# Values of the decode rows: plain float32 products, four batches to four quarters of the PSUM partitions

## The chip, the cores and the metric

The kernel runs on one core of a Trainium2 chip. The time is the device time of one execution in microseconds (us), and lower is better. Three executions were timed and one more was profiled.

## What is computed

One layer of a hybrid decoder is run on a prompt of 1024 tokens and on 32 decode rows (8 batches of 4 new tokens). Both go through one input projection, a state-space branch with a gated linear unit, and an attention branch of 8 heads of 64 columns; the two branches are normalised and multiplied by `w_out`. The part that matters here is the attention of the decode rows over the cached keys and values, which is three dilated windows for each new token:

```python
def _dilated_gather(q, k_all, v_all, window, dil):
    ...
    kg = k_all[:, idx_c]
    vg = v_all[:, idx_c]
    s = jnp.einsum('bthe,btkhe->bhtk', q, kg) * (HEAD_DIM ** -0.5)
    ...
    p = jnp.exp(s - m[..., None])
    l = jnp.sum(p, axis=-1)
    o = jnp.einsum('bhtk,btkhe->bthe', p, vg)
    return o, m.transpose(0, 2, 1), l.transpose(0, 2, 1)
```

All inputs and results are float32.

## The kernel before

TensorE multiplies in a fast reduced form, float32r. To keep accuracy the kernel splits most operands into a high part (ScalarE copies into a float32r tile) and a low part (VectorE or GpSimd subtract the high part from the source), and adds up two or three products of parts. Names that end in `h` and `l`, or `hi` and `lo`, are such parts. A few small products are done on plain float32 tiles instead.

The program has four stages: the input projection with the state-space blocks; the gated unit with the decode rows' scores; a stretch in which three jobs are mixed; and a last stage in which the attention half of the output projection is done for eight slices of the prompt. The change is in the third stage, whose three jobs are:

- The prompt's attention heads, 8 of them. For each, TensorE makes scores (`ss`, L1518), VectorE adds a mask and finds row extremes (`pm`, `mn`, L1521), ScalarE takes exponentials (L1533), GpSimd divides (L1541), TensorE transposes (`tp`, L1560), ScalarE and VectorE make parts (`ph`, L1564, and `pl`, L1567), and TensorE multiplies them with the values (`ops`, L1575). A head has 10 micro steps of transposes and products.
- The ssm half of the output projection (`fo`, L1670), 32 groups of 6 matmuls.
- The values of the decode rows, in `values_ops`. For each of 8 batches there are 6 tiles of 128 cached rows by 512 columns (`ct`, 256 KB each), loaded from `cache_v` by `cache_tile`. ScalarE makes `vh` (L1355), VectorE and GpSimd in turn make `vl` (L1359), and TensorE multiplies the softmax weights `st6` of this batch and tile with both (L1365). The weights hold high and low parts side by side: 2 parts x 4 tokens x 8 heads are 64 columns, so that a batch's result is 64 x 512 in a PSUM bank. A product makes all 8 heads' columns for each head's weights; `mask` (L1377) keeps the right ones, `pick` (L1381) adds up two batches' rows with the constant matrix `selb` into a 32 x 512 tile, and VectorE adds that to `yad` (L1386).

The order of instructions on TensorE, VectorE, ScalarE and GpSimd in this stage is that of `Plan.run`: each step has an engine, a cost in microseconds, a priority, steps that it depends on, and tokens (buffers) that it takes and gives. A list schedule over these costs gives the order in which the steps are written. `CT`, `VH` and `VL` are the numbers of `ct`, `vh` and `vl` buffers. SyncE (the queue `SP`) issues all transfers in the order of the program; the transfers' engine is `DM` in the plan. The softmax weights `st6` are written in `decode_ops` by `his`, `los` and `far` before the values begin; zeros in them are set by GpSimd.

Of the kernel before, what the change touches and what calls it, by code (L numbers as in the profile page):

```python
# [103 lines left out]
def hymba_kernel(ctx: ExitStack, tc: tile.TileContext, I, O):  # L104
# [29 lines left out]
    def f(t):  # L134
        return t.bitcast(F32)
# [974 lines left out]

    CT, VH, VL, LEAD = 5, 2, 1, 6
    d3 = ExitStack()
    early = maskp = d2 = hmask = st6 = yad = sc = None

    def open_decode():
        nonlocal early, maskp, d2, hmask, st6, yad, sc
        rst.close()
        dst.close()
        fin[0] = None
        early = ctx.enter_context(tc.tile_pool(reuse_waits="tile", name="early", bufs=1))  # L1120
        maskp = early.tile([128, 1024], F32, name="maskp")
        SY.dma_start(maskp, I["c_maskp"])
        d2 = dec[0] = dst.enter_context(tc.tile_pool(reuse_waits="tile", name="d2", bufs=1))
        hmask = d2.tile([128, 512], F32, name="hmask")
        SY.dma_start(hmask, I["c_hmask"])
        st6 = d2.tile([128, 6, DB, 2, DS, H], F32R, name="st6")
        yad = d2.tile([NT, 512], F32, name="yad")
        sc = d3.enter_context(tc.tile_pool(reuse_waits="tile", name="d3", bufs=1)).tile([64, DS, 292], F32, name="sc")

    def decode_ops(t0, dt_, opened):  # L1130
# [10 lines left out]
        o.q, o.k, o.v = newr  # L1141
        z6 = op(PO, 1.8, lambda: GP.memset(f(st6[:, 2:6]), 0.0), t0, [opened])
        shn = [64, 2, DS, E]
# [77 lines left out]
        def his(k):  # L1221
            def fn():
                if k == 0:
                    S.activation(by_batch(st6[:, 0, :, 0]), o.pv, AF.Copy)
                else:
                    for j in range(DS):
                        S.activation(st6[:, 2 + j, :, 0, j, :], o.pv[:, j], AF.Copy)
            return fn

        def los(k):  # L1230
            def fn():
                if k == 0:
                    V.tensor_tensor(out=by_batch(st6[:, 0, :, 1]), in0=o.pv, in1=f(by_batch(st6[:, 0, :, 0])), op=OP.subtract)
                else:
                    for j in range(DS):
                        V.tensor_tensor(out=st6[:, 2 + j, :, 1, j, :], in0=o.pv[:, j], in1=f(st6[:, 2 + j, :, 0, j, :]), op=OP.subtract)
            return fn

        for k in range(2):
            step(PE, 0.2, turn(k), take=["fo"])  # L1240
            step(AC, 0.4 + 0.5 * k, his(k), deps=[last[0], z6])
            step(VE, 0.4 + 0.2 * k, los(k), give=["fo"])

# [9 lines left out]

        def far():
            o.far = row()[:, :256].rearrange("p (j n) -> p j n", j=DS)
            V.tensor_tensor(out=o.far, in0=o.p.unsqueeze(1).to_broadcast([128, DS, 64]),
                            in1=sel3.unsqueeze(2).to_broadcast([128, DS, 64]), op=OP.mult)
            o.far = o.far.rearrange("p j (b h) -> p j b h", h=H)
        step(VE, 0.3, far, give=["fo"], take=["dm"])
        step(AC, 0.4, lambda: S.activation(by_batch(st6[:, 1, :, 0]), o.far, AF.Copy))  # L1260
        step(VE, 0.4, lambda: V.tensor_tensor(out=by_batch(st6[:, 1, :, 1]), in0=o.far, in1=f(by_batch(st6[:, 1, :, 0])), op=OP.subtract),
             give=["dm"])
        return o

    def own_ops(o, t0):
# [3 lines left out]
        def own(u):  # L1269
            def fn():  # L1270
                if u == 0:
                    o.on = gk([128, 512], "vh", bufs=VH)[:64, :256].rearrange("p (j e) -> p j e", e=E)
                r = slice(2 * u, 2 * u + 2)
# [63 lines left out]
    def values_ops(t0, dt_, own, sel):  # L1337

        o = Box()
        o.c, o.vh, o.vl, o.po = {}, {}, {}, {}  # L1340
        end = own
        prev = lows = None
        for b in range(DB):
            if b % 2 == 0:
                w = Box()
            for t in range(6):
                n = 6 * b + t
                pr = t0 + n * dt_

                def load(b=b, t=t, n=n):  # L1350
                    o.c[n] = cache_tile(cv, b, t)

                def vhi(n=n):
                    o.vh[n] = gk([128, 512], "vh", F32R, VH)
                    S.activation(o.vh[n], o.c[n], AF.Copy)  # L1355

                def vlo(n=n, e=GP if n % 2 else V):
                    o.vl[n] = gk([128, 512], "vl", F32R, VL)
                    e.tensor_tensor(out=o.vl[n], in0=o.c[n], in1=f(o.vh[n]), op=OP.subtract)  # L1359

                def mm(b=b, t=t, n=n):
                    if t == 0:
                        o.po[b] = fo_ps([64, 512])
# [4 lines left out]
                a = op(DM, 0.75, load, pr - 2, [], take=["ct"])  # L1368
                a = op(AC, 0.52, vhi, pr - 0.5, [a], take=["vh"])
                lows = op(PO if n % 2 else VE, 1.23 if n % 2 else 0.6, vlo, pr - 0.5, [a, lows if VL == 1 else None], take=["vl"], give=["ct"])  # L1370
                prev = op(PE, 0.43, mm, pr, [lows, prev], take=["fo"] if t == 0 else [], give=["vh", "vl"])


            def mask(b=b, w=w):
                if b % 2 == 0:
                    w.m = row()
                V.tensor_tensor(out=w.m[64 * (b % 2):64 * (b % 2) + 64], in0=o.po[b], in1=hmask[:64], op=OP.mult)  # L1377

            def pick(g=b // 2, w=w):
# [3 lines left out]
            a = op(VE, 0.6, mask, pr, [prev], take=[] if b % 2 else ["dm"], give=["fo"])  # L1383
            if b % 2:
                a = op(PE, 0.85, pick, pr, [a, sel], take=["kt"], give=["dm"])
                end = op(VE, 0.6, lambda w=w: V.tensor_tensor(out=yad, in0=w.yd, in1=yad, op=OP.add), pr, [a, end], give=["kt"])  # L1386

        def zin():
            o.z, o.g = row(NT), gk([128, 512], "vh", bufs=VH)[:NT]
            SY.dma_start(o.z, d_pd.rearrange("j b c -> (j b) c")[:, 2560:3072])  # L1390
# [34 lines left out]

    selb = gp.tile([128, DB // 2, NT], F32, name="selb")

# [221 lines left out]
    def out_ssm_ops(t0, dt_):  # L1649
# [3 lines left out]
        for s in range(8):  # L1653
# [9 lines left out]
            for u in range(2):  # L1663
                for hf in range(2):
# [22 lines left out]

    plan.tokens = {**BANKS, "pp": 8, "ct": CT, "vh": VH, "vl": VL, "dm": 1, "nv": 1, "ko": 1, "q": 3, "ka": 2,
                   "vs": 2, "mn": 4, "dn": 4, "rd": 4, "ph": 2, "yp": 3, "gt": 1, "st": 2, "gh": 2,
# [91 lines left out]
def _constants():  # L1781
# [18 lines left out]
    col = np.arange(NT)[None, None, :]  # L1800
    batch = 2 * np.arange(DB // 2)[None, :, None] + r[:, None, None] // 64
    selb = ((r[:, None, None] // 8 % 4 == col // 8) & (batch == col % 8)).astype(np.float32)
# [81 lines left out]
```

## Time and profile before

| what | value |
|---|---|
| time, median of 3 runs | 741.25 us (740.29 to 742.72) |
| the profiled execution's own time | 745.36 us |
| its span in the profile | 743.6 us |
| TensorE busy in the span (PE) | 683.3 us, 92% |
| VectorE (DVE) | 564.1 us, 76% |
| ScalarE (ACT) | 366.8 us, 49% |
| GpSimd (POOL) | 348.0 us, 47% |
| mean transfer rate | 159 GB/s |

A busy share of TensorE includes the time in which a matmul runs out of its pipeline while the next one is already in it, so 92% is not 92% of its peak. PEld is the weight load of TensorE, which overlaps its matmuls. Times in the rows below are from the start of the span.

### The profile page before, as it was taken

The page shows a single profiled execution, that of the slowest core. Times are in us where ns is not written, and L with a number is a line of the kernel's source. Part 1 is how long each engine was busy: PE and PEld are TensorE (multiplying, and loading weights), DVE is VectorE, ACT ScalarE, POOL GpSimd, SP SyncE. Part 2 cuts the span into 40 slices and gives each one's busy share as a digit, 9 for nine tenths or more (in the row PEclk, how much of TensorE's full clock was granted, in tenths as well). Part 3 has the DMA queues.
Part 4 walks back from the last instruction along what each step waited for, and adds up shares of the span by engine and source line. Part 5 has one row for each costly group of instructions (what it writes and reads, how often), then busy time and mean ns, then how long its engine had stood idle before and what let it go on. Part 6 is the DMA issues. An engine that isn't in the chain of part 4 may idle for free.

```text
span 743.6 us, 12795 instructions
## 1 busy us (share of the span) xinstructions
PE 683.3 (92%) x4286; PEld 623.8 (84%) x4286; DVE 564.1 (76%) x1249; ACT 366.8 (49%) x814; POOL 348.0 (47%) x315
## 2 busy tenths in 40 slices
PE   7999989779798899999899999889999989898995
PEld 5999979679798889999899899668777768786995
DVE  5997858777978687346687687598899999974584
ACT  6663242514234355244343324277788878762442
POOL 2326456445564632203575750056788778430041
PEclk9999988979899999999989999999999999997998
DMA  8612432222224243277866745598998686116032
GB/s 280 202 57 82 145 99 76 78 95 61 73 90 126 80 153 94 92 248 259 261 203 186 243 135 193 161 298 275 262 300 242 202 254 178 41 58 229 19 120 114
DMA packets 78034, 118.38 MB, mean 159 GB/s; under 512 B 15216, under 2 KB 43376, under 8 KB 77968
## 3 DMA queue, kind: packets, MB, share of 16 engines
q1 hardware_dynamic: 77968, 117.56, 50.0%
q8 instruction: 34, 0.56, 0.3%
q14 instruction: 32, 0.26, 0.1%
HBM read 85.73 MB, written 30.62 MB: 156 GB/s over the span
## 4 chain that ended last, share of the span: by engine, by line
PE 51%; DVE 24%; DMA 8%; issue 6%; ACT 5%; POOL 5%; SPq 1%; DVEq 0%; POOLq 0%; ACTq 0%
PE mm L314 13%; PE mm L294 6%; PE fo L1670 4%; PE ss L294 3%; PE tp L294 3%; PE ops L1575 3%; DVE pm L1521 3%; POOL dm L977 3%; PE so L685 3%; PE tp L1560 2%; DVE vl L1359 2%; PE ss L1518 2%; DVE pl L1567 2%; PE fo L1365 2%; DVE win L143 2%
## 5 line engine op out<-in xcount | busy, mean ns | idle before, releaser
L314 PE MATMUL mm<-xT,win 128*128 128x352 f32 x1008 | 178.1, 334 | 15.1 <-DVE eq L381 13.7
L314 PEld LDWEIGHTS mm<-xT,win 128*128 128x128 f32 x1008 | 168.2, 196 | 16.8 <-issue 14.0
L1022 PE MATMUL mm<-xT,win 128*128 128x352 f32 x432 | 76.4, 331 | 0.4 <-DVE win L1004 0.2
L977 POOL TENSOR_TENSOR dm<-ct,dq 128x512 f32<-128x512 f32 x40 | 52.8, 1350 | 46.6 <-DMA ct<-in_cache_k_dram 27.6
L1022 PEld LDWEIGHTS mm<-xT,win 128*128 128x128 f32 x432 | 70.5, 192 | 1.1 <-DVE win L1004 0.9
L1541 POOL TENSOR_SCALAR pm<-pm,rd 128x128 f32<-128x128 f32 (+3 forms) x64 | 51.0, 803 | 32.2 <-DVE rd L1537 27.7
L1533 ACT ACTIVATE pm<-pm,mn 128x128 f32<-128x128 f32 (+3 forms) x64 | 49.3, 772 | 13.2 <-DVE mn L1521 12.1
L294 PE MATMUL mm<-win,xT 128*128 128x256 f32 x384 | 51.7, 290 | 0.1
L1567 DVE TENSOR_TENSOR pl<-tp,ph 128x512 fp32r<-128x512 f32 (+1 forms) x80 | 49.4, 627 | 3.0 <-ACT ph L1564 2.9
L1670 PE MATMUL fo<-wo,gh 128*128 128x512 f32 x192 | 51.0, 406 | 0.3 <-DVE yp L1597 0.3
L809 PE MATMUL gl<-yh,wg 128*128 128x272 f32 (+1 forms) x256 | 50.8, 297 | 0.0
L294 PEld LDWEIGHTS mm<-win,xT 128*128 128x128 f32 x384 | 48.1, 194 | 0.5 <-ACT xT L139 0.4
L1564 ACT ACTIVATE ph<-tp 128x512 fp32r<-128x512 f32 (+1 forms) x80 | 43.1, 547 | 8.1 <-PE tp L1560 7.0
L1560 PE MATMUL tp<-ident,pm 128*128 128x128 f32 x288 | 45.1, 275 | 0.5 <-DVE mn L1521 0.5
L143 DVE SCALAR_TENSOR_TENSOR win<-wst,gin,win 128x256 fp32r<-128x256 f32 x72 | 43.9, 650 | 1.9 <-ACT win L142 1.4
L809 PEld LDWEIGHTS gl<-yh,wg 128*128 128x128 f32 x256 | 41.9, 198 | 0.0
L1670 PEld LDWEIGHTS fo<-wo,gh 128*128 128x128 f32 x192 | 35.4, 193 | 7.4 <-DVE yp L1597 0.6
L1521 DVE CUSTOM_DVE_ANT_0 pm<-ss,maskp 128x512 f32<-128x512 f32 (+2 forms) x64 | 36.6, 580 | 6.0 <-PE ss L1518 5.9
L1560 PEld LDWEIGHTS tp<-ident,pm 128*128 128x128 f32 x288 | 34.4, 141 | 6.4 <-DVE mn L1521 1.4
L980 DVE TENSOR_REDUCE scd<-dm 128x8 f32<-128x512 f32 x40 | 26.9, 680 | 15.9 <-POOL dm L977 15.8
L1518 PE MATMUL ss<-ka,qt 128*128 128x512 f32 (+2 forms) x96 | 36.1, 378 | 2.5 <-DMA ka<-d_k 1.8
L809 PE MATMUL gl<-yl,wg 128*128 128x272 f32 (+1 forms) x128 | 37.6, 294 | 0.0
(411 smaller groups left out, 1648.6 us busy)
## 6 DMA issues: line engine op xcount, KB each, us to landing
wst<-in_w_in_dram SPq DMA_DIRECT2D x24, 512.0 KB
ct<-in_cache_k_dram SPq DMA_DIRECT2D x48, 256.0 KB
ct<-in_cache_v_dram SPq DMA_DIRECT2D x48, 256.0 KB
xt<-in_x_prompt_dram SPq DMA_DIRECT2D x8, 512.0 KB
wst<-in_w_out_dram SPq DMA_DIRECT2D x8, 512.0 KB
xres<-in_x_prompt_dram SPq DMA_DIRECT2D x8, 512.0 KB
qt<-d_q SPq DMA_DIRECT2D x16, 256.0 KB
qw<-d_q SPq DMA_DIRECT2D x32, 128.0 KB
```

The source lines that it names most:

```text
L143: V.scalar_tensor_tensor(lo, src, scale, f(hi), op0=OP.mult, op1=OP.subtract)
L294: T.matmul(out, lhs(a, kt), w(b, kt)[:, c0:c0 + cn], start=(n == 0), stop=(n == 3 * ktn - 1))
L314: T.matmul(p, w(b, kt)[:, c * 128:c * 128 + 128], x(a, kt), start=(n == 0), stop=(n == 23))
L809: T.matmul(p, wg[:, b, kt, c:c + 128], o.y[a][:, kt, :, :o.w], start=(n == 0), stop=(n == 11))
L977: GP.tensor_tensor(out=y.m, in0=y.c, in1=x.q, op=OP.mult)
L1022: T.matmul(x.p, o.w[kt][:, b, c * 128:c * 128 + 128], xT[a][:, kt, 352 * k:352 * k + 352], start=(kt == 0 and j == 0), stop=(kt == 7 and j ...
L1518: T.matmul(x.p[c][:, :w], q[:, i % 4 * 128:i % 4 * 128 + 128], o.ka[:, 512 * c:512 * c + w], start=(m == 0), stop=(m == 1))
L1521: V.tensor_tensor_reduce(out=x.pm[:, 512 * c:512 * c + w], in0=x.p[c][:, :w], in1=maskp[:, (7 - i) * 128 + 512 * c:(7 - i) * 128 + 512 * c ...
L1541: a = op(PO, 0.02 + n * 0.0012, lambda: GP.tensor_scalar(x.pm[:, :n], x.pm[:, :n], x.rd, 1.0, op0=OP.mult, op1=OP.mult), pr, [a], give=["rd"])
L1560: T.transpose(x.p[:, n * 128:n * 128 + 128], o.rows[2 * m + u].pm[:, j * 128:j * 128 + 128], ident)
L1567: V.tensor_tensor(out=x.l[:, :w], in0=x.p[:, :w], in1=f(x.h[:, :w]), op=OP.subtract)
L1670: T.matmul(o.f[hf], o.g[u][:, i, k], wo[0][:, j, 2 * u + k, hf * 512:hf * 512 + 512], start=(u + k + n == 0), stop=(u + k + n == 4))
```

## The change

The softmax weights `st6` are kept in one part, as plain float32: 4 tokens x 8 heads are 32 columns for a batch and tile. The values tiles are multiplied as they come, without `vh` and `vl`. Four batches are taken together: batch 4g + b writes partitions 32b to 32b + 31 of one PSUM bank, so that there are 2 groups of batches with 6 tiles each, 12 steps of four products, in place of 48 steps of two. `mask` now works on 128 partitions, and there are 2 masks, picks and additions in place of 8, 4 and 4. `selb` and its constant follow. `CT` goes from 5 to 8, and the tokens of `vl` are gone.

```diff
-    CT, VH, VL, LEAD = 5, 2, 1, 6
+    CT, LEAD = 8, 6
...
-        st6 = d2.tile([128, 6, DB, 2, DS, H], F32R, name="st6")
+        st6 = d2.tile([128, 6, DB, DS, H], F32, name="st6")
...
-            step(VE, 0.4 + 0.2 * k, los(k), give=["fo"])
+            step(AC, 0.4 + 0.5 * k, his(k), deps=[last[0], z6], give=["fo"])
...
-        step(AC, 0.4, lambda: S.activation(by_batch(st6[:, 1, :, 0]), o.far, AF.Copy))
-        step(VE, 0.4, lambda: V.tensor_tensor(out=by_batch(st6[:, 1, :, 1]), in0=o.far, in1=f(by_batch(st6[:, 1, :, 0])), op=OP.subtract),
-             give=["dm"])
...
-                def vhi(n=n):
-                    o.vh[n] = gk([128, 512], "vh", F32R, VH)
-                    S.activation(o.vh[n], o.c[n], AF.Copy)
...
-                    e.tensor_tensor(out=o.vl[n], in0=o.c[n], in1=f(o.vh[n]), op=OP.subtract)
...
-                    for u, x in enumerate((o.vh[n], o.vl[n])):
-                        T.matmul(o.po[b], st6[:, t, b].rearrange("p u j h -> p (u j h)"), x,
-                                 start=(t == 0 and u == 0), stop=(t == 5 and u == 1))
...
-                prev = op(PE, 0.43, mm, pr, [lows, prev], take=["fo"] if t == 0 else [], give=["vh", "vl"])
...
+                        w.po = fo_ps([128, 512])
+                    for b in range(4):
+                        T.matmul(w.po[32 * b:32 * b + 32], st6[:, t, 4 * g + b].rearrange("p j h -> p (j h)"), o.c[b, t, g],
+                                 start=(t == 0), stop=(t == 5))
+
+                prev = op(PE, 2.2, mm, pr, [*loads, prev], take=["fo"] if t == 0 else [], give=["ct"] * 4)
...
+                V.tensor_tensor(out=w.m, in0=w.po, in1=hmask, op=OP.mult)
```

On TensorE, at the first values products of the stretch, the order before is this (a pair of products for one tile, between pieces of the first head; `wo` and `gh` are the output projection):

```order
L1575 MATMUL ops<-pl,vs 128x256 x2
L1365 MATMUL fo<-vh,st_5314 64x512
L1365 MATMUL fo<-vl,st_5314 64x512
L1560 MATMUL tp<-ident,pm_5714 128x128
...
L1670 MATMUL fo<-wo_4987,gh 128x512 x6
L1365 MATMUL fo<-vh,st_5314 64x512
L1365 MATMUL fo<-vl,st_5314 64x512
L1518 MATMUL ss<-ka,qt 128x512
```

And this is the order of the changed program around its first pick, that is from the end of the first half of the batches to the second step of the second half (L1340 is the values product, L1352 the pick, L1640 the projection, L1488 the scores):

```order
L1352 MATMUL kt<-dm,selb 32x512
L1340 MATMUL fo<-ct,st_5314 32x512 x4
L1640 MATMUL fo<-wo_4987,gh 128x512 x6
L1488 MATMUL ss<-ka,qt 128x512
L1488 MATMUL ss<-ka,qw 128x512
L1640 MATMUL fo<-wo_4987,gh 128x512 x6
L1488 MATMUL ss<-ka,qt 128x128
L1488 MATMUL ss<-ka,qw 128x128
L1340 MATMUL fo<-ct,st_5314 32x512 x4
```

Products that came in pairs all through the stretch now come four at a time. The last values product stood behind 61 of the 80 micro steps, and stands behind 33 of them now; the projection groups ahead of it were 24 of 32 and are 15.

On SyncE's queue, from the first values load, the order before is this (`qt`, `qw` and `ka` are a head's queries and keys, `nv` its values, `d_h` a store of projected rows):

```order
L890 DMA ct<-in_cache_v_dram 128x512
L1463 DMA ka<-d_k 128x512
L892 DMA ct<-in_cache_v_dram 128x1x512
L1453 DMA qt<-d_q 128x512
L1454 DMA qw<-d_q 64x512
L1455 DMA qw<-d_q 64x512
L894 DMA ct<-in_cache_v_dram 128x512
```

And in the changed program, from the same place:

```order
L890 DMA ct<-in_cache_v_dram 128x512 x4
L1433 DMA ka<-d_k 128x512
L1423 DMA qt<-d_q 128x512
L1424 DMA qw<-d_q 64x512
L1425 DMA qw<-d_q 64x512
L1667 DMA selb<-in_c_selb_dram 128x64
L892 DMA ct<-in_cache_v_dram 128x1x512 x4
L1433 DMA ka<-d_k 128x512
L1414 DMA nv<-d_v 128x1024
L1656 DMA d_h<-xres 128x512
L894 DMA ct<-in_cache_v_dram 128x512 x4
```

Four loads stand together now, one for each batch of a group, and the loads of a head stand between such fours.

## Rows read from the trace of the kernel before

**Rows 1.** Windows: busy us (and instructions) of each engine, granted clock, transfers.

```profile
core 0: us, PE busy (x) PEld busy (x) DVE busy (x) ACT busy (x) POOL busy (x), PEclk, DMA share, GB/s
472.10:492.50 20.40, 17.09 (x84) 13.31 (x83) 15.15 (x44) 10.22 (x25) 8.24 (x10) 1.00 0.88 260
492.50:565.00 72.50, 68.85 (x421) 56.69 (x419) 64.19 (x161) 56.45 (x121) 51.15 (x44) 1.00 0.92 280
565.00:640.00 75.00, 71.23 (x433) 56.69 (x433) 71.85 (x179) 60.81 (x131) 59.35 (x54) 1.00 0.67 202
640.00:665.20 25.20, 22.78 (x145) 20.19 (x143) 23.28 (x63) 18.15 (x39) 8.95 (x9) 0.93 0.12 34
665.20:679.00 13.80, 10.92 (x59) 9.51 (x59) 4.70 (x8) 3.07 (x6) 1.30 (x1) 0.82 0.27 91
679.00:743.60 64.60, 56.98 (x225) 52.40 (x224) 37.66 (x100) 25.13 (x59) 11.10 (x8) 0.92 0.33 123
```

**Rows 2.** TensorE's groups by line, 472 to 680 us: busy, mean ns | idle before.

```profile
L1670 PE MATMUL fo<-wo,gh 128*128 128x512 f32 x192 | 51.0, 406 | 0.3 <-DVE yp L1597 0.3
L1560 PE MATMUL tp<-ident,pm 128*128 128x128 f32 x288 | 45.1, 275 | 0.5 <-DVE mn L1521 0.5
L1518 PE MATMUL ss<-ka,qt 128*128 128x512 f32 (+2 forms) x96 | 36.1, 378 | 2.5 <-DMA ka<-d_k 1.8 <-DMA qt<-d_q 0.5 <-DVE mn L1521 0.2
L1575 PE MATMUL ops<-pl,vs 128*128 128x256 f32 (+1 forms) x160 | 34.8, 300 | 1.7 <-DVE pl L1567 1.6
...
L1381 PE MATMUL kt<-dm,selb 128*32 128x512 f32 x8 | 4.2, 604 | 0.0
L1630 PE MATMUL kt<-ones,sq 128*64 128x1 f32 x32 | 4.2, 259 | 3.2 <-DVE sq L1625 3.2
```

**Rows 3.** Pieces of the chain of waits: start us, us, what.

```profile
515.92 0.46 PE ss L1518 x2
516.38 0.46 PE ops L1575 x4
517.17 0.47 PE fo L1365 x2
665.21 2.08 PE kt L1630 x16
671.37 2.75 PE fo L1670 x12
```

**Rows 4.** TensorE in order of time around a pick: start us, us.

```profile
529.10 0.60 PE L1560 MATMUL tp<-ident,pm 128*128 128x128 f32 x4
...
530.23 0.40 PE L1518 MATMUL ss<-ka,qw 128*128 128x512 f32 x1
530.56 1.04 PE L1381 MATMUL kt<-dm,selb 128*32 128x512 f32 x2
531.53 0.44 PE L1365 MATMUL fo<-vh,st 128*64 128x512 f32 x1
```

**Rows 5.** Waits of TensorE's weight loads, 490 to 640 us: us, times, longest.

```profile
PEld fo L1365 <- DVE vl L1359: 8.1, 9, 2.1
...
PEld ops L1575 <- DVE pl L1567: 2.4, 4, 0.9
```

**Rows 6.** Groups by line that the change removes or cuts, 490 to 640 us.

```profile
L1359 POOL TENSOR_TENSOR vl<-ct,vh 128x512 fp32r<-128x512 f32 x24 | 31.8, 1324 | 9.3 <-ACT vh L1355 4.2 <-issue 2.9 <-ACT gh L1302 1.8
L1355 ACT ACTIVATE vh<-ct 128x512 fp32r<-128x512 f32 x48 | 29.9, 623 | 8.0 <-PE fo L1365 3.3 <-DMA ct<-in_cache_v_dram 3.2 <-DVE vl L1359 1.1
L1359 DVE TENSOR_TENSOR vl<-ct,vh 128x512 fp32r<-128x512 f32 x24 | 25.8, 1077 | 0.2
L1377 DVE TENSOR_TENSOR dm<-fo,hmask 64x512 f32<-64x512 f32 x8 | 5.4, 680 | 0.2
```

**Rows 7.** The first values load's issue, and (min/median/max ns, first and last start) its copies.

```profile
484.18 0.58 SPq L890 DMA_DIRECT2D ct<-in_cache_v_dram x1
L1355 ACT ACTIVATE vh<-ct x48: 614/620/636, 490.4 to 625.5; 128x512 fp32r<-128x512 f32 x48
```

More of the change, by code (lines that the diff above doesn't have):

```diff
@@ L1141, in decode_ops @@
         o.q, o.k, o.v = newr
-        z6 = op(PO, 1.8, lambda: GP.memset(f(st6[:, 2:6]), 0.0), t0, [opened])
+        z6 = op(PO, 0.9, lambda: GP.memset(st6[:, 2:6], 0.0), t0, [opened])
         shn = [64, 2, DS, E]
@@ L1223, in fn @@
                 if k == 0:
-                    S.activation(by_batch(st6[:, 0, :, 0]), o.pv, AF.Copy)
+                    S.activation(by_batch(st6[:, 0]), o.pv, AF.Copy)
                 else:
                     for j in range(DS):
[L1227 to L1236, printed above, removed]
+                        S.activation(st6[:, 2 + j, :, j, :], o.pv[:, j], AF.Copy)
             return fn
@@ L1252, in decode_ops @@
         step(PE, 0.11, turn3, take=["fo"], give=["dm"])
[L1254 to L1259, printed above, removed]
-        step(AC, 0.4, lambda: S.activation(by_batch(st6[:, 1, :, 0]), o.far, AF.Copy))
-        step(VE, 0.4, lambda: V.tensor_tensor(out=by_batch(st6[:, 1, :, 1]), in0=o.far, in1=f(by_batch(st6[:, 1, :, 0])), op=OP.subtract),
-             give=["dm"])
+        step(VE, 0.4, lambda: V.tensor_tensor(out=by_batch(st6[:, 1]), in0=o.p.rearrange("p (b h) -> p b h", h=H).unsqueeze(1).to_broadcast([128, DS, DB, H]),
+                                              in1=sel3.unsqueeze(2).unsqueeze(3).to_broadcast([128, DS, DB, H]), op=OP.mult), give=["fo"])
         return o
@@ new lines, in values_ops, with load, mm, mask @@
+        o.c = {}
+        end, prev = own, None
+        for g in range(DB // 4):
+            w = Box()
+            for t in range(6):
+                pr, loads = t0 + (24 * g + 4 * t) * dt_, []
+                for b in range(4):
+                    def load(b=b, t=t, g=g):
+                        o.c[b, t, g] = cache_tile(cv, 4 * g + b, t)
+                    loads.append(op(DM, 0.75, load, pr - 3 + b * 0.2, [], take=["ct"]))
+                def mm(g=g, t=t, w=w):
+                    if t == 0:
+                        w.po = fo_ps([128, 512])
+                    for b in range(4):
+                        T.matmul(w.po[32 * b:32 * b + 32], st6[:, t, 4 * g + b].rearrange("p j h -> p (j h)"), o.c[b, t, g],
+                                 start=(t == 0), stop=(t == 5))
+                prev = op(PE, 2.2, mm, pr, [*loads, prev], take=["fo"] if t == 0 else [], give=["ct"] * 4)
+            def mask(w=w):
+                w.m = row()
+                V.tensor_tensor(out=w.m, in0=w.po, in1=hmask, op=OP.mult)
+            def pick(g=g, w=w):
@@ L1380, in pick @@
                 w.yd = kt_ps([NT, 512])
                 T.matmul(w.yd, selb[:, g], w.m, start=True, stop=True)
[L1383 to L1386, printed above, removed]
+            a = op(VE, 0.6, mask, pr, [prev], take=["dm"], give=["fo"])
@@ L1388, in zin @@
+            a = op(PE, 0.85, pick, pr, [a, sel], take=["kt"], give=["dm"])
+            end = op(VE, 0.6, lambda w=w: V.tensor_tensor(out=yad, in0=w.yd, in1=yad, op=OP.add), pr, [a, end], give=["kt"])
         def zin():
-            o.z, o.g = row(NT), gk([128, 512], "vh", bufs=VH)[:NT]
+            o.z, o.g = row(NT), gk([128, 512], "vh")[:NT]
             SY.dma_start(o.z, d_pd.rearrange("j b c -> (j b) c")[:, 2560:3072])
@@ L1424, in hymba_kernel @@
     gp = pat.enter_context(tc.tile_pool(reuse_waits="tile", name="gp", bufs=1, side="right"))
-    selb = gp.tile([128, DB // 2, NT], F32, name="selb")
+    selb = gp.tile([128, DB // 4, NT], F32, name="selb")
     def gk(shape, name, dt=F32, bufs=1):
@@ L1800, in _constants @@
     col = np.arange(NT)[None, None, :]
[L1801 removed]
+    batch = 4 * np.arange(DB // 4)[None, :, None] + r[:, None, None] // 32
     selb = ((r[:, None, None] // 8 % 4 == col // 8) & (batch == col % 8)).astype(np.float32)
```

27 lines of the change are left out of this document (2 added, 25 removed).

## The prediction

> **What bounds the kernel now.** I read the windows first, to find where the change acts [rows 1]. The decode rows' values start at 492.5 us, inside a stretch that does three jobs at once: attention heads, the ssm half of the output projection, and decode values. It opens at 472.1 us with the first projection product and ends at 679.0 us, 206.9 us in all. TensorE is busy 95% of the time from 492.5 to 640 us and VectorE 92%, so neither is clearly alone. A busy share hides the pipeline, so I counted TensorE's work by its pace, from the groups by line [rows 2] and the pieces of the chain of waits [rows 3]: 192 projection matmuls at 2.75/12 = 0.229 us make 44.0. The scores' 192 are of several widths; a head has 36 blocks of 128 columns, twice, or 18 matmuls of 512; 144 of these at 0.23 make 33.1. The 320 products with probabilities are 36 x 8 = 288 of 256 columns, at 0.46/4 = 0.115: 33.1. The 288 transposes are (0.60 - 0.275)/3 = 0.108 apart [rows 2, 4]: 31.1. The 48 pairs of values (one to each `vh` copy [rows 6]) at 0.47: 22.6. Four picks, each of 0.97 from its start to the next start [rows 4]: 3.9. Two batches of sums at 2.08: 4.2. Together 172.0 of 206.9 us.
>
> Before the first values matmul there are some 15.5 us of that work (7 projection groups of 6, 11 scores, 10 transposes, 2 products, counted in the program's order), and the sums are the end after 665.2. So from 492.5 to 665.2 there are 172.0 - 15.5 - 4.2 = 152.3 us of TensorE work in 172.7 us: 20.4 us are lost. The list of waits says to what [rows 5]: TensorE's weight loads waited 8.1 us for `vl`, the low parts of the values tiles, and 2.4 us for `pl`, VectorE's low parts of the probabilities. The rest are waits under a microsecond each and pipeline gaps that no row names. TensorE's work therefore sets the stretch, and VectorE's lateness adds to it.
>
> **What the change removes.** From ScalarE 48 copies (29.9 us), from GpSimd 24 subtractions (31.8), from VectorE 24 more (25.8) and, since a mask now takes 128 partitions, six of eight masks at 0.68 (4.1) [rows 6]. None of these 92 us comes off the time by itself, since TensorE's work goes on beside them. What comes off are TensorE's waits on them: all 8.1 us for `vl`. Of the 2.4 us for `pl` and of like waits below a microsecond (for `mn`, `yp`) I take 2.5 us as gone, since VectorE, busy 159.3 us of 172.7 in those three windows, falls by some 30 us. Bounds: 0 (the order hands the freed slots to work that waits anyway) and 9 (three quarters of the 20.4 - 8.1 that are left). One part of `st6` instead of two saves six VectorE subtractions before the values start; they stood beside the last input projection's matmuls, and I cost them at nothing. Without that cover they would give back at most 6 x 0.68 = 4.1 us, each priced as a mask. Everything after 679 us is untouched.
>
> **What it adds.** 48 pairs at 0.47 go, 12 groups of four plain float32 products come. The only such product in the stretch is the pick, 128x32 weights over 512 columns [rows 4]: one instruction of the program shows as two records; they span 1.04 us and one takes 0.604, so the second starts 0.43 after the first. Pace: 2 x 0.43 = 0.86 against 0.235 for one part product today. The pick also starts 0.33 after its neighbour, 0.10 more than the 0.23 pace, and holds the engine 0.97, 0.11 more than 0.86: 0.21 to go into and out of the narrow form. A group of four is eight records. If they follow each other, a group takes 8 x 0.43 + 0.21 = 3.65; if all four products overlap fully, 2 x 0.43 + 0.21 = 1.07. No row of this trace has neighbouring matmuls in different quarters of the output, so the value between is a choice. The two records of one product share a quarter and cannot overlap, while the second record of one and the first of the next lie in different quarters and can. In program order that makes five steps: 5 x 0.43 + 0.21 = 2.36, the middle of the two bounds. 12 x 2.36 = 28.3 against 22.6: +5.7. Bounds 12.8 (-9.8) and 43.8 (+21.2). Two of four picks fall away: -2 x (0.97 + 0.10) = -2.1; their additions on VectorE too, at no price.
>
> The Trainium skill, "TensorE: Matmul & The Clock Gate", section "Part 3: Packing small matmuls", says that matmuls in different column tiles start about 4 ns apart and still in program order. Program order is what my five steps use; the 4 ns alone, without the two records of one product, would give the 1.07 us group (rival B). Another of its pages speaks against the change: "FP8 and Floating Point Precision", section "TensorE Precision Notes", counts four passes for true float32, and the pick's pace agrees (0.86 is 3.7 times 0.235). By that alone, without overlap, the sum would be the serial one (rival C).
>
> **What is late next.** A values product now waits for the loads of four tiles and for nothing else. The wait stands on TensorE's own queue, so all matmuls behind it wait, and behind them ScalarE's copies of transposes. SyncE issues in order: four loads sit together, and behind them the heads' `qt`, `qw` and `ka`. The transfer engines are 92% busy at 280 GB/s to 565 us [rows 1], about 304 GB/s when full. By the issues in the new order, 22.9 MB go out from the first values load to the last; at 304 GB/s that is 75 us. The new order puts 76 us of TensorE's work between the first and the last group (projections 8 groups, 33 of 80 micro steps, 11 values groups), some 86 us at its present use (152.3 of 172.7). So the loads about keep up. Before, the first load was issued at 484.2 us and its copy began at 490.4 [rows 7], 6.2 us later. With eight tile buffers the loads of a group wait for the group two before. The tightest place is the seventh group (the second half's first), 5.9 us of TensorE work behind the fifth one's end: there the wait is perhaps 1 us, with as much for the first group and as much for all others: +3. Bounds 0 and 11 (about 1 us for each of the 12 groups).
>
> **The sum.** -8.1 - 2.5 + 5.7 - 2.1 + 3.0 = -4.0 us, against the profiled execution's 745.4 us (its span of 743.6 and 1.8 around it): 741.4. That execution is 0.6% above the median of the three runs, 741.25; carried over, 737.3 us.
>
> **Rivals.** A, the above: five steps per group, chance 0.47, 732 to 743 by the bounds of waits alone. B, full overlap, chance 0.17: the group is 1.07, so 15.5 us less than A; but then TensorE needs only 76 - 14 = 62 us between the first and the last values group, 70 at its present use, where the loads take 75. At least those 5 us come back as waits for `ct`, and since the groups are spread unevenly I take 8: 729.8. For it speaks that nothing but the pair in one quarter ties the records; against it, that the records stand in one queue. C, on the other side: no overlap, chance 0.22. The group is 3.65, 15.5 more than A; the loads then have time, which saves A's 3: 749.8. It is slower from 3.0 us a group on, where A's gain of 4.0 plus the 3.0 of waits is eaten. For it speaks that the rows have never shown two matmuls in the array at once in this kernel; against it, nothing but the output's quarters. D, also slower, chance 0.14: the groups pace as in A, but the loads come late. A load took 6.2 us at a busy place, and a group now needs the last of four. If the groups wait 1.2 us each, or 14 in all, the time is 737.3 + 11 = 748. It is no gain from 0.6 us a group on.
>
> **How the numbers follow.** 0.3% of 741.25 is 2.2 us, about what can be told from no change. Faster (below 739.0): most of A (0.33) and B, 0.50. Same (to 743.5): 0.10 of A, and the near edges of C and D, 0.14. Slower: what is left, 0.36. The range runs from just below B's value to just above C's, 728 to 751, which leaves out the far halves of B and C and little else.
>
> **What would show it.** In the changed profile the values products should be 96 records of some 0.6 us, two to a product. A span of eight near 2.3 us with starts in pairs confirms A, 3.6 us C, 1.1 us B. `vh` and `vl` conversions are gone, and VectorE's share in the stretch drops to about three quarters. Waits of TensorE's queue for `ct` add up to about 3 us; above 10 it is D. The stretch after the last sum stays at 64.6 us. I am wrong if the 20.4 us of lost TensorE time are not due to VectorE at all, or if the order, which now finishes the values at about micro step 33 of 80 instead of 61, starves the heads at either end.

## The result, and the profile after

The changed kernel takes 736.8 us (median of 9 runs, 730.3 to 740.4) against 741.4 us for the kernel before on the same chip (9 runs, 740.2 to 743.4). The ratio is 0.9911, with a 95% interval of 0.9887 to 0.9935; by the ratio it is 6.6 us faster, 4.8 to 8.4, while the two medians are 4.6 us apart. The profiled execution took 736.8 us, with a span of 735.0. The forecast was 737.3 us. The time came out as forecast, but two terms of the sum were far off and cancelled each other; the experiments show which.

The windows of the changed kernel answer to [rows 1]; the first row is the whole stretch, the second the last stage, and the other two the part with the values products.

```profile
core 0: us, PE busy (x) PEld busy (x) DVE busy (x) ACT busy (x) POOL busy (x), PEclk, DMA share, GB/s
472.10:672.80 200.70, 186.34 (x1130) 148.37 (x1130) 151.74 (x418) 121.09 (x268) 94.00 (x92) 0.97 0.68 211
672.80:735.00 62.20, 54.59 (x224) 51.19 (x224) 36.90 (x100) 24.99 (x59) 11.13 (x8) 0.96 0.36 135
...
494.00:530.00 36.00, 33.31 (x200) 20.92 (x198) 22.01 (x55) 16.16 (x35) 10.97 (x11) 1.00 0.97 320
530.00:575.00 45.00, 41.63 (x266) 30.65 (x265) 32.78 (x99) 29.65 (x65) 23.00 (x23) 1.00 0.94 300
```

The stretch took 200.7 us, where it took 206.9 before. VectorE is busy 151.7 us of it, 76% (the forecast said three quarters). The last stage took 62.2 us instead of 64.6, with the same 224 matmuls and a mean granted clock of 0.96 instead of 0.92; in the profile of a repeat of the changed kernel it took 63.7, of which more below. Between 494 and 530 us the transfer engines are 97% busy at 320 GB/s: that is where the values are loaded, and they are full.

TensorE's groups by line in the stretch, which answer to [rows 2] (L1340 is the values product, L1352 the pick, L1378 the transposes of `yad`; the share after the bar is idle time ahead of the group and what ended it):

```profile
L1640 PE MATMUL fo<-wo,gh 128*128 128x512 f32 x192 | 51.9, 415 | 0.0
L1530 PE MATMUL tp<-ident,pm 128*128 128x128 f32 x288 | 45.8, 277 | 2.2 <-POOL pm L1511 1.2 <-DVE mn L1491 0.9
L1488 PE MATMUL ss<-ka,qt 128*128 128x512 f32 (+2 forms) x96 | 36.9, 385 | 3.1 <-DMA ka<-d_k 2.7 <-DVE rd L1507 0.2
L1545 PE MATMUL ops<-pl,vs 128*128 128x256 f32 (+1 forms) x160 | 35.2, 302 | 0.7 <-DVE pl L1537 0.7
...
L1340 PE MATMUL fo<-ct,st 128*32 128x512 f32 x96 | 18.5, 604 | 2.7 <-DMA ct<-in_cache_v_dram 2.7
...
L1352 PE MATMUL kt<-dm,selb 128*32 128x512 f32 x4 | 2.1, 604 | 1.1 <-DVE dm L1348 1.1
...
L1378 PE MATMUL fo<-ident,yad 32*128 32x32 f32 x4 | 0.6, 295 | 4.3 <-DVE pl L1537 4.3
```

The 96 records of some 0.6 us are there, two to a product. 96 x 0.604 would be 58 us, yet the group was busy for 18.5: the records overlap. How far, the timeline shows (start, duration; the piece in brackets is idle time ahead of it). The first row is a group whose tiles had landed, with the start of what follows it; the other two are groups whose tiles came late:

```profile
494.41 1.07 PE L1340 MATMUL fo<-ct,st 128*32 128x512 f32 x8
495.41 0.50 PE L1488 MATMUL ss<-ka,qt 128*128 128x512 f32 x1
...
523.51 3.02 PE L1340 MATMUL fo<-ct,st 128*32 128x512 f32 x8 [2.05 <-DMA ct<-in_cache_v_dram]
...
529.34 2.38 PE L1340 MATMUL fo<-ct,st 128*32 128x512 f32 x8
...
566.61 1.07 PE L1340 MATMUL fo<-ct,st 128*32 128x512 f32 x8
```

A group of four products spans 1.07 us, and the next instruction starts 1.00 after it: full overlap, not the five steps (2.36 us) of the forecast. Groups that are longer are so because their four tiles land one by one.

The waits of TensorE's weight loads from 492 to 660 us answer to [rows 5]:

```profile
PEld fo L1340 <- DMA ct<-in_cache_v_dram: 7.6, 9, 2.3
PEld ss L1488 <- issue: 5.0, 6, 0.8
PEld fo L1378 <- DVE pl L1537: 4.5, 1, 4.5
PEld ops L1545 <- ACT ph L1534: 2.5, 3, 0.8
...
PEld ops L1545 <- DVE pl L1537: 1.4, 4, 0.7
```

The 8.1 us for `vl` are gone, and the wait for `pl` ahead of the heads' products fell from 2.4 to 1.4. In their place stand 7.6 us for the loads of values tiles. The matmuls themselves stood 2.7 us for these loads, in three places (2.05 us of it at 523.51, above), but that is the same idle time seen on the other list and is not to be added. One new wait of 4.5 us stands ahead of `yad`'s transposes.

### The profile page after: what moved, and what is told of

Its sections match the earlier page's. It is cut to its first block, busy times and chain, and to the rows that moved or that the text cites. A ratio compares the mean times of both kernels' runs of the same rounds, so it can differ in the third digit from the quotient of the medians.

```text
span 735.0 us, 12713 instructions
## 1 busy us (share of the span) xinstructions
PE 669.6 (91%) x4282; PEld 607.0 (83%) x4282; DVE 534.1 (73%) x1211; ACT 338.2 (46%) x765; POOL 313.7 (43%) x291
## 4 chain that ended last, share of the span: by engine, by line
PE 47%; DVE 19%; DMA 14%; issue 6%; ACT 6%; POOL 5%; SPq 3%; DVEq 0%; ACTq 0%; POOLq 0%
PE mm L314 10%; PE mm L294 5%; PE fo L1640 4%; PE ops L1545 4%; PE ss L294 3%; PE tp L294 3%; PE mm L1022 3%; PE ss L1488 3%; PE tp L1530 3%; PE so L685 2%; POOL dm L977 2%; DMA wst<-in_w_in_dram 2%; DMA d_k<-eq 2%; DMA ct<-in_cache_v_dram 2%; PE fo L1340 2%
## 5 line engine op out<-in xcount | busy, mean ns | idle before, releaser
L1511 POOL TENSOR_SCALAR pm<-pm,rd 128x128 f32<-128x128 f32 (+3 forms) x64 | 49.4, 777 | 62.5 <-DVE rd L1507 47.3
L1640 PE MATMUL fo<-wo,gh 128*128 128x512 f32 x192 | 51.9, 415 | 0.0
L809 PE MATMUL gl<-yh,wg 128*128 128x272 f32 (+1 forms) x256 | 48.5, 288 | 0.0
L1640 PEld LDWEIGHTS fo<-wo,gh 128*128 128x128 f32 x192 | 36.7, 200 | 8.0 <-issue 0.8
L809 PEld LDWEIGHTS gl<-yh,wg 128*128 128x128 f32 x256 | 39.9, 189 | 0.0
L1488 PE MATMUL ss<-ka,qt 128*128 128x512 f32 (+2 forms) x96 | 36.9, 385 | 3.1 <-DMA ka<-d_k 2.7
```

The costliest lines, as they stand in the source:

```text
L809: T.matmul(p, wg[:, b, kt, c:c + 128], o.y[a][:, kt, :, :o.w], start=(n == 0), stop=(n == 11))
L1488: T.matmul(x.p[c][:, :w], q[:, i % 4 * 128:i % 4 * 128 + 128], o.ka[:, 512 * c:512 * c + w], start=(m == 0), stop=(m == 1))
L1511: a = op(PO, 0.02 + n * 0.0012, lambda: GP.tensor_scalar(x.pm[:, :n], x.pm[:, :n], x.rd, 1.0, op0=OP.mult, op1=OP.mult), pr, [a], give=["rd"])
L1640: T.matmul(o.f[hf], o.g[u][:, i, k], wo[0][:, j, 2 * u + k, hf * 512:hf * 512 + 512], start=(u + k + n == 0), stop=(u + k + n == 4))
```

## The experiments

In all of them the time is compared by its ratio to the kernel before, run beside it on the same chip, and a difference between two kernels is the difference of their ratios times 741.4 us. The ratio of the changed kernel is 0.9911.

**All products in one quarter.** From the second tile on, all four products of a group write the first quarter (the other batches' rows then hold their first tile alone):

```diff
-                        T.matmul(w.po[32 * b:32 * b + 32], ..., start=(t == 0), stop=(t == 5))
+                        q = b if t == 0 else 0
+                        T.matmul(w.po[32 * q:32 * q + 32], ..., start=(t == 0), stop=(t == 5 and b == 3 or t == 0 and b > 0))
```

> The changed kernel, but from the second tile step of each half on, all four products of a group go to the first quarter of the PSUM partitions (so the rows of the other three batches hold only their first tile's part). Theory F (products in different quarters overlap fully, so a group costs TensorE about 1.0 us, and the loads of the values tiles hold it up): ten of the twelve groups become serial, 8 x 0.43 us each, 2.5 us more, +24 us of TensorE work, of which some 8 us is taken back from the waits for the loads: 753 us (748 to 758), and a span of eight records near 3.5 us. Rival R (the gain is what VectorE, ScalarE and GpSimd no longer do; what the products cost TensorE hides beside them): 737 to 743 us.

Measured: 748.1 us, ratio 1.0061 (1.0037 to 1.0085), which is 745.9 us by the ratio, between the two ranges. A group in this kernel's timeline, its line being L1341:

```profile
500.21 3.62 PE L1341 MATMUL fo<-ct,st 128*32 128x512 f32 x8
503.76 0.66 PE L1531 MATMUL tp<-ident,pm 128*128 128x128 f32 x4
```

The quarters are what makes the overlap: 3.55 us from start to the next start in one quarter, 1.00 in four. Ten groups so lengthened are 25.5 us more of TensorE's work, but the time rose by 11.1 us only. TensorE's work is thus not worth its full length in time; the waits for `ct` fell to 1.6 us of weight loads in this kernel's list, so part of the lengthening stood where the changed kernel waited.

**Eight loads in place of 48.** Only the first two tiles of the first four batches are loaded, and all products read those; the order on the engines is the same (10.5 MB of loads and most of the values are left out):

```diff
-                        o.c[b, t, g] = cache_tile(cv, 4 * g + b, t)
+                        if g == 0 and t < 2:
+                            o.c[b, t, g] = cache_tile(cv, 4 * g + b, t)
```

> The changed kernel in the same order on TensorE, VectorE, ScalarE and GpSimd, but only the first 8 of the 48 values tiles are loaded and all twelve groups read these (so the values are wrong, and 10.5 MB of transfers are left out). Theory F: TensorE's waits for the tiles, 10.3 us in the changed kernel, go, and a few waits for the heads' own loads with them: 725 us (721 to 729). Rival R (the loads are hidden, TensorE would have waited for the heads in any case): 734 to 738 us.

Measured: 726.8 us, ratio 0.9772 (0.9746 to 0.9797), 10.3 us faster than the changed kernel (uncertainty 2.6), as theory F expected. The expectation had its own 10.3 us by adding the weight loads' 7.6 us and the matmuls' 2.7, which are the same waits; so either the loads cost more than their listed waits, such as by holding up the heads' own loads, or the match is luck. The groups by line from 472 to 680 us, and two windows:

```profile
L1341 PE MATMUL fo<-ct,st 128*32 128x512 f32 x96 | 13.6, 604 | 0.0
```

```profile
494.00:530.00 36.00, 36.00 (x239) 24.98 (x238) 26.61 (x66) 18.27 (x40) 12.96 (x12) 1.00 0.76 231
530.00:575.00 45.00, 43.02 (x286) 33.50 (x286) 37.87 (x113) 33.76 (x77) 29.49 (x29) 1.00 0.64 185
```

No values product waits any more, and in the first window TensorE has no idle time and does 239 instructions instead of 200. By this run the loads cost the changed kernel 10.3 us, not 3.0.

**Values spread out.** The step of priority from one values tile to the next is 1.2 instead of 0.7555, so that the last product stands behind 52 of the 80 micro steps instead of 33.

> The changed kernel with the priority step of the values raised from 0.7555 to 1.2 per tile, so that the last values product stands behind 52 of the 80 micro steps and not behind 33; nothing else changes. Theory F: the loads get half as much time again for the same bytes, the waits for them fall from 10 us to 3 or less: 729 us (725 to 733). Rival R, or if what is lost is due to the heads and not to the loads: 735 to 740 us.

Measured: 739.4 us, ratio 0.9932 (0.9907 to 0.9957), which is 736.4 us by the ratio: no gain over the changed kernel, as rival R expected. Its waits of weight loads from 472 to 690 us:

```profile
PEld ops L1545 <- ACT ph L1534: 7.0, 5, 3.6
PEld tp L1530 <- POOL pm L1511: 5.4, 1, 5.4
PEld ops L1545 <- DVE pl L1537: 5.2, 9, 1.0
...
PEld fo L1340 <- DMA ct<-in_cache_v_dram: 1.8, 4, 0.5
```

The waits for `ct` fell from 7.6 to 1.8 us, and waits for the heads' steps took their place. The transfer engines were as full as before from 494 to 530 us (1.00 of the time). The windows do not say that the heads' own loads caused all of it; that they are late is seen in the chain of waits, where `qt` now stands with 3.3% of the span and had 2.7% in the changed kernel.

**Conversions put back, read by nobody.** 48 copies and 48 subtractions on a constant tile, first close to the values products:

```diff
+                    conv[b % 2] = op(AC, 0.52, hi, pr - 0.5, [conv[b % 2]])
+                    conv[b % 2] = op(PO if b % 2 else VE, 1.23 if b % 2 else 0.6, lo, pr - 0.5, [conv[b % 2]])
```

> The changed kernel, with 48 copies on ScalarE and 24 subtractions each on VectorE and GpSimd put back, of the old shape, but from a constant tile into two tiles that nobody reads: the engines' old work without TensorE's waits on it. Theory F: this work costs what VectorE's lateness brings back to the waits for the heads, 2 to 5 us: 740 us (738 to 743). Rival R (the relief of the three engines is the whole gain): back to the time before, 741 to 746 us, and TensorE's waits for pl, mn and ph grow by more than 5 us.

Measured: 749.8 us, ratio 1.0082 (1.0055 to 1.0109), 12.7 us above the changed kernel, more than either theory allowed. Since the products had moved into the first half of the stretch and took the conversions along, they were repeated with priorities spread as in the kernel before, (24g + 4t + b) x 1.3 in place of pr - 0.5:

> The 48 copies and 48 subtractions are put back on ScalarE, VectorE and GpSimd, on constant data into tiles that nobody reads, with priorities that spread them over the stretch as they were spread in the kernel before; no product waits for them. Theory R (taking them away gave TensorE only waits worth a few us, as predicted, 2.5 us, and the 12.7 us of the packed copy came from their density): 737 to 741. Rival P (their mere presence on VectorE delays the heads' steps by some 10 us however they stand): 745 to 750.

Measured: ratio 1.0135 (1.0104 to 1.0165), 16.6 us above the changed kernel. Spreading did not help; theory R is refuted, and at 751.4 us by the ratio rival P's range is passed as well. Then the same without VectorE's 24 subtractions:

> The spread idle conversions without VectorE's 24 subtractions: 48 copies on ScalarE and 24 subtractions on GpSimd stay, read by nobody. Theory V (VectorE's time is what the conversions cost): no more than 3 us above the changed kernel, 737 to 741. Rival G (ScalarE's and GpSimd's steps hold up the heads as well, by their place in the queues): half or more of the 12 to 15 us stays, 743 to 750.

Measured: ratio 1.0001 (0.9970 to 1.0031), 6.7 us above the changed kernel. Theory V is refuted. Rival G is nearer: of 12.7 and 16.6 us, 6.7 stay with GpSimd's subtractions and ScalarE's copies. The other 9.9 (uncertainty 3.2) go with VectorE's subtractions; the two spread kernels ran on different chips, each against its own kernel before. The waits of weight loads in the spread kernel with all conversions, from 472 to 690 us (L1558 are the heads' products, L1550 `pl`, `cv` the idle tile):

```profile
PEld ops L1558 <- DVE pl L1550: 10.9, 11, 2.9
PEld fo L1341 <- DMA ct<-in_cache_v_dram: 6.4, 8, 2.4
...
PEld fo L1391 <- DVE pl L1550: 3.8, 1, 3.8
PEld ops L1558 <- ACT cv L1347: 3.4, 4, 0.8
```

The conversions delay the heads' `pl` on VectorE, and TensorE waits for that, 10.9 us instead of 1.4. In the same stretch ScalarE's idle copies stood for VectorE's subtractions, since each works in a tile that the other must be done with:

```profile
ACT cv L1347 <- DVE cv L1350: 9.5, 8, 2.3
```

In the kernel before, the copies stood 1.1 us for `vl` [rows 6]. So the idle conversions are not quite the old ones: they hold up ScalarE too, at a price that was not tried.

**The kernel before, without conversions.** The opposite direction: ScalarE copies one column of a loaded tile in place of 512, nothing is subtracted, and both products of a pair read one of two tiles that are converted once (the decode rows' values are left out). Pairs, masks and picks are those of before:

```diff
-                    o.vh[n] = gk([128, 512], "vh", F32R, VH)
-                    S.activation(o.vh[n], o.c[n], AF.Copy)
+                    if n < 2:
+                        o.vh[n] = gk([128, 512], f"cv{n}", F32R, 1)
+                        S.activation(o.vh[n], o.c[n], AF.Copy)
+                    else:
+                        S.activation(o.vh[n % 2][:, :1], o.c[n][:, :1], AF.Copy)
...
-                    for u, x in enumerate((o.vh[n], o.vl[n])):
+                    for u, x in enumerate((o.vh[n % 2], o.vh[n % 2])):
...
-                lows = op(PO if n % 2 else VE, 1.23 if n % 2 else 0.6, vlo, ...)
```

> The kernel before, without the conversions of values: ScalarE copies one column of a loaded tile instead of 512 (so that the product still waits for the load), nothing is subtracted, and both products of a pair read a constant tile (the decode rows' values are left out of the result). 48 pairs, eight masks and four picks stay as in the kernel before. The plan orders it much like the changed kernel. Theory T (TensorE's work sets the stretch): the 48 pairs cost 22.6 us where twelve groups cost 13, and two picks more 2.1, but the waits for loads shrink by what the pairs cover; so slower than the changed kernel by 3 to 8 us, about 740 to 745. Rival R (what the change gave came from the conversions' removal, and TensorE's own work has slack): as fast as the changed kernel, 735 to 738.

Measured: 737.9 us, ratio 0.9926 (0.9896 to 0.9956). That is 1.1 us above the changed kernel, with an uncertainty of 2.8: not told apart, as rival R expected. Its plan ends the values behind 36 of 80 micro steps, much as in the changed kernel. So most of what the change gave in time comes without any plain product. The stretch alone is less clear: from its first projection product to its last sums it took 202.7 us in this kernel's profile, and 200.6 and 197.9 us in the two profiles of the changed kernel, while its start differs by 2 to 3 us. So with the loads on, the plain products can be worth some 1 to 5 us. Why the plain products add so little is asked by the next one: the same kernel with two tiles loaded in place of 48 (12.1 MB left out).

> The kernel without conversions, with 48 pairs, of which now only the first two values tiles are loaded (12.1 MB of loads and the decode rows' values are left out; TensorE's order is the same but for a few rows at the end of the stretch). It stands to the kernel of plain products with eight loads (ratio 0.977) as the kernel without conversions stands to the changed kernel. Theory W (the plain products save 11.7 us of TensorE's work, which the loads hide as long as they run): without the loads the difference shows, 0.985 to 0.995. Rival V (TensorE's work has slack even then, since VectorE's and the heads' steps set the pace): within 0.003 of it, 0.974 to 0.980.

Measured: 732.7 us, ratio 0.9857 (0.9827 to 0.9888), against 0.9772 for the plain products with eight loads. Without the loads the plain products are worth 6.3 us (uncertainty 2.9), below the 11.7 of work that the expectation put on them but outside what rival V allowed; theory W's range holds the ratio, at its lower end. The step between the two kernels also takes six masks from VectorE and the short copies from ScalarE and changes the order somewhat, so that 6.3 us is not TensorE's work alone. The waits of weight loads in the kernel without conversions, with all its loads (L1368 is the values product, which here waits for the short copy `cv` of a loaded tile, and so for the load behind it):

```profile
PEld fo L1368 <- ACT cv L1358: 5.9, 8, 1.8
PEld ops L1577 <- DVE pl L1569: 4.5, 11, 1.5
```

and with two loads (no row of the values product is among the longest):

```profile
PEld ops L1578 <- DVE pl L1570: 3.7, 8, 1.5
PEld ss L1521 <- issue: 3.3, 3, 1.6
PEld kt L1633 <- DVE sq L1628: 1.9, 1, 1.9
```

**Three attempts to gain more.** The first books the measured costs in the plan, 1.05 us for a group and 1.1 for a load.

> The plan books 1.05 us for a group of four products (as measured, in place of 2.2) and 1.1 us for a load of a values tile (in place of 0.75). In the order, 12 projection groups now stand between the first and the last values group in place of 8, some 5.5 us more of TensorE's work while the loads run. Theory W (TensorE waits for the loads, and any work put beside them shortens the wait by as much): the waits for ct fall by about 5 us and the time with them, 732 us (730 to 735). Rival M (as in the spread kernel, what is taken from the waits for ct comes back as waits for the heads' own loads and steps): 736 to 739.

Measured: ratio 0.9994 (0.9963 to 1.0025), 6.2 us above the changed kernel. In its list the weight loads wait 6.8 us for `ct`, little less than 7.6, and 5.8 us, once, ahead of the sums; its profiled execution, 748.3 us, is the slowest of its 12, whose median is 741.7. Both expectations missed.

The second moves `yad`'s transposes behind two more micro steps.

```diff
+        pr += 12
         a = op(PE, 0.3, turn, pr, [a], take=["fo"])
```

> yad's four transposes (and the parts made of them) get a priority later by 12, so that two micro steps and eight scores more stand on TensorE ahead of them. Theory T (TensorE stands 4.3 us because the transposes are in its queue before yad's chain of six steps is done, and nothing else waits there): the wait goes and the time falls by 3 to 4.3 us, 732.5 to 734. Rival H (the stretch from 575 us on is bound by VectorE and the heads' steps, which work on during that wait, so that another wait takes its place): no change, 736 to 738.

Measured: ratio 0.9998 (0.9975 to 1.0021), 6.5 us above the changed kernel; both missed again. The waits of its matmuls from 575 to 690 us (L1546 are the heads' products, L1601 the sums; its profiled execution took 738.1 us, the median of its runs is 742.3), and then those of the changed kernel:

```profile
PE ops L1546 <- DVE pl L1538: 5.6, 4, 4.1
PE kt L1601 <- DVE sq L1596: 4.1, 1, 4.1
```

```profile
PE fo L1378 <- DVE pl L1537: 4.3, 1, 4.3
PE kt L1352 <- DVE dm L1348: 1.1, 1, 1.1
PE ops L1545 <- DVE pl L1537: 0.5, 1, 0.5
```

The wait of 4.3 us did not go. It stands now ahead of the heads' next products, again with VectorE as the last to come, and a further 4.1 us ahead of the sums. `yad`'s transposes were only the place where TensorE met VectorE's lateness, which is rival H's mechanism; the price above rival H's "no change" is not explained by these lists.

The third takes CT from 8 to 10.

> CT is 10 in place of 8, so that the loads of a group can be issued earlier, half of them while the group before is still unread. Theory W (the waits for ct come from the rate of the transfer engines, full at 320 GB/s from 494 to 530 us): no change, 735.5 to 738. Rival N (they come from too few buffers: the loads of the sixth group were issued at 515.6 us, when the fourth group's tiles came free): faster by 3 us or more, 730 to 734.

Measured: ratio 0.9976 (0.9943 to 1.0009), 4.8 us above the changed kernel, with 13.3 us of waits for `ct` in the weight loads' list. More buffers did not shorten the waits, so nothing speaks for rival N. Theory W's "no change" missed as well: the plan also moved its steps, and what made it slower was not pursued.

**The changed kernel again**, since the last three had a scattered comparison:

> The changed kernel as it is, once more, beside the two kernels below and on the same chip, since the four kernels before stood against a kernel before that scattered over 10 us. If the ratio of 0.991 holds on every chip: 0.989 to 0.994. If the gain is lost on a chip with a slower or more uneven transfer rate: 0.995 to 1.000.

Measured: 737.7 us, ratio 0.9912 (0.9883 to 0.9942). The ratio holds on this chip. It does not settle the other three: they ran on another chip, together with the spread idle conversions and without the changed kernel, so a smaller gain on that chip is a rival that was not tested. For a real loss it speaks that their stretches, from the first projection product to the last sums, took 206.9, 203.8 and 203.8 us in their profiles, against 200.6 and 197.9 for the changed kernel. No variant that does the whole work was measured faster than it.

## Why the forecast came out, term by term

**Waits for `vl` and VectorE's relief, -8.1 and -2.5: right in kind, not shown in size.** The waits for `vl` are gone, and the idle conversions show that VectorE's share delays the heads. The kernel without conversions and with two loads is 10.6 us faster than before (0.9857, 8.3 to 12.8), the very sum of both terms, and it has the pairs, masks and picks of before. But it also leaves out 12.1 MB of loads and has a changed order, and no run takes the loads out of the kernel before. With its loads on it is 5.5 us faster (0.9926), and conversions put back cost 12.7 and 16.6 us. So the price lies between some 5 and 17 us and hangs on what stands beside them; that 10.6 met 10.6 is luck as far as the runs show. Why it is higher when they are put back stays open, but for ScalarE's waits on the idle tiles.

**The values products, +5.7, and the picks, -2.1: the first is the step that failed.** "In program order that makes five steps" was wrong: eight records in four quarters take 1.00 us from start to next start, rival B's 1.07 within 7%. Twelve groups are 12.0 us of work against 22.6, so the term was -10.6 and not +5.7, and with the picks -12.7. By what the Trainium skill says in "TensorE: Matmul & The Clock Gate", section "Part 3: Packing small matmuls", on starts some 4 ns apart, the group would be the 1.07 us of rival B, and the trace agrees; the runs show that this holds for products of two records as well. By the four passes that the Trainium skill counts in "FP8 and Floating Point Precision", section "TensorE Precision Notes", four products one after the other would take some 4 x 4 x 0.235 = 3.8 us (an estimate), and the group in one quarter roughly agrees with 3.62; that section does not speak of products in different quarters. The forecast's serial price from its own rows, 3.65, was met. In time, the products and picks gave 6.3 us where no loads stood in the way (0.9857 to 0.9772), and 1.1, which cannot be told from nothing, where they did (0.9926 to 0.9911; up to 5 by the stretches in the profiles).

**The loads, +3.0: mis-sized, 10.3 by the run without most of them.** "So the loads about keep up" rested on 76 us of TensorE's work between the first and the last group, which held the products at 2.36. At 1.00 it is 76 - 11 x 1.36 = 61 us, while the products ran from 494.4 to 571.9 us, 77.5 us, against the 75 us that were worked out for the transfers. The transfers set this part, as the run with eight loads shows, and the chain of waits has two long pieces of loads in it:

```profile
506.97 4.78 DMA ct<-in_cache_v_dram
511.80 1.04 PE fo L1340 x2
515.57 7.90 DMA ct<-in_cache_v_dram
523.51 3.02 PE fo L1340 x8
```

A load is on the chain for 7.9 us here, where one took 6.2 before [rows 7]. Rival B had this mechanism and 8 us for it.

**The two errors, one against the other.** By the ratios: -10.6 for the conversions, -6.3 for products and picks, +10.3 for the loads, in all -6.6. By the forecast: -10.6, +3.6, +3.0, in all -4.0. The measured three add up by construction, since each is the step from one kernel to the next (before, no conversions and two loads, plain products and eight loads, changed); on another path, with the loads on, they are -5.5 and -1.1. On the first path the products were 9.9 us too dear and the loads 7.3 too cheap. That is no accident of unrelated terms: what TensorE saves inside the 77.5 us it hands to the loads' wait. The group in one quarter shows it, whose 25.5 us more of work cost 11.1 while the waits for `ct` fell from 7.6 to 1.6. The kernel without conversions shows the same from the other side: its pairs, with 22.6 us of work where the groups have 12.0, lose only 5.1 us to the loads (0.9926 to 0.9857) where the plain products lose 10.3.

**The rest.** "TensorE's work therefore sets the stretch" does not hold where the loads are on after the change: 25.5 us more of that work cost 11.1. "Everything after 679 us is untouched" was off by 2.4 us in the first profile of the changed kernel (62.2 us at a mean granted clock of 0.96, where it took 64.6 at 0.92) and by 0.9 in that of the repeat (63.7 at 0.93). Windows show the difference. Before (last sums, 16 products of one column each, from 677.0 to 679.1 us):

```profile
673.00:677.00 4.00, 1.13 (x6) 0.59 (x5) 2.62 (x4) 2.06 (x3) 1.15 (x1) 1.00 0.29 82
678.00:683.00 5.00, 5.00 (x18) 3.75 (x19) 3.65 (x10) 1.15 (x1) 0.00 (x0) 0.50 1.02 330
683.00:685.00 2.00, 2.00 (x7) 1.10 (x6) 0.67 (x4) 0.00 (x0) 0.00 (x0) 0.66 1.04 409
```

The changed kernel (its two blocks of such sums from 659.6 to 661.7 and from 670.7 to 672.8 us):

```profile
662.00:665.00 3.00, 3.00 (x10) 2.42 (x10) 0.68 (x1) 0.59 (x1) 0.95 (x1) 0.50 0.00 0
672.80:676.80 4.00, 4.00 (x17) 2.95 (x18) 3.21 (x13) 0.00 (x0) 0.00 (x0) 1.00 0.92 297
```

And its repeat (last sums from 667.0 to 669.1 us):

```profile
667.00:669.00 2.00, 2.00 (x17) 1.98 (x16) 0.75 (x1) 0.02 (x1) 0.00 (x0) 1.00 0.88 213
670.00:673.00 3.00, 3.00 (x8) 1.89 (x8) 2.50 (x9) 0.00 (x0) 0.00 (x0) 0.50 0.89 333
```

A clock of 0.50 is the lower of its two levels (1.2 and 2.4 GHz). Before, TensorE stood 2.9 us ahead of its last sums, and the lower level lasted some 6.8 us, from within the sums into the last stage. In the changed kernel nothing stands there, and yet the lower level comes, for some 3.4 us: in the first profile behind the first block of sums, inside the stretch, and in the repeat behind the last one, where the last stage pays. So the last stage differs between two executions of one kernel as well. The other profiles agree: in the five more where TensorE stood 2.9 to 5.6 us ahead of the last sums the lower level lasted 6.8 us or longer, without idle time there it was 3.4 us or none, and with about 1.5 us of it 3.4 us twice and 6.8 once. So a pause that a denser order closes seems to give back more than its own length; no run changed the pause alone. The worry about heads starved by a denser order showed as one wait, 4.3 us at `yad`'s transposes, which a shift of the order moves and does not remove.

## What to carry to other kernels

Products with 32 output columns in plain float32 are cheap when four of them go to the four quarters of a PSUM bank, and dear one after the other. Before such a saving is booked, the bytes that the same part must load are divided by the rate that the transfers reach when full: if that time is longer than the work that is left, the saving turns into a wait. And when a forecast meets the time, each term still wants a run of its own, such as one with the loads taken out; here two terms were off by some 7 and 10 us under a total that was off by less than one by the medians and by 2.5 by the ratio (734.8 us).

## What had not been expected of the hardware

Eight records of 592 to 618 ns each, in four quarters of the output, took 1.00 us from the first start to the next instruction's, and 3.55 us in one quarter: 3.5 times. The length of a record tells nothing of it; only the span of the group does. Small changes of the order (four transposes moved by two micro steps, two more buffers, two costs in the plan) each came out 4.8 to 6.5 us above the changed kernel, about what the change gave, on a chip on which that kernel itself was not run. TensorE's granted clock fell to 0.50 behind a block of one-column sums, for some 3.4 us without idle time ahead of the block and for some 6.8 us with 2.9 us of it.
